# Loading k, its row factors and y two tiles ahead, with six buffers for partial sums, in a hybrid attention and state-space layer

## The chip, the cores and the metric

The kernel runs on one core of one Trainium2 chip. The metric is device time in microseconds (us), the median of several executions; less is better. The core has five engines: TensorE (PE) multiplies matrices, VectorE (DVE), ScalarE (ACT) and GpSimd (POOL) work on tiles of 128 partitions, and SyncE (SP) issues every transfer between device memory (HBM) and the on-chip memory. Each engine works through its own queue in order and waits on semaphores for the others, so an instruction that waits holds up everything behind it on the same engine.

## The reference

One decoder layer on x of 1024 rows and 2048 columns, all in float32:

```python
h = rms_norm(x, ln_gain)
q, k, v, z_att, u, z_ssm, g_att, g_ssm = split(h @ w_in)      # widths 6 x 1024, 2 x 2048
q, k = rms_norm of q and k over each group of 64 channels
attn = (softmax(q1 k1') - lam * softmax(q2 k2')) v            # causal, 8 heads, two maps per head
y_att = rms_norm(attn) * (1 - lam_init) * silu(z_att)
y = gelu(S5 state-space scan of u);  y_ssm = y * sigmoid(y @ w_glu + b_glu) * silu(z_ssm)
merged = sigmoid(g_att) * (y_att @ w_proj_att) + sigmoid(g_ssm) * (y_ssm @ w_proj_ssm)
out = x + merged @ w_out
```

## The kernel before

**Precision.** TensorE multiplies in a rounded float32 format, so each operand is split into a high part (an ACT copy that rounds, L90) and a low part (a DVE subtraction, L91), and a product is three matmuls: high by high, high by low, low by high.

**The input projection.** `h @ w_in` is made in pairs of 128-column blocks: one *pair* gives two blocks of 128 output channels by two halves of 512 rows, that is four result tiles of 128x512. It is done with seven block products in place of eight (a Strassen-Winograd scheme, `pair`, L503 and on). A product is 12 matmuls of 512 columns (L497), so a pair is 84. DVE and ACT make the sums of weight blocks (L346, L366), their high and low parts, and copy or combine the results (u1, u2, u3, p1; L515 to L532, L580 to L591). The contraction of 2048 runs in two halves: a first pass over the 36 pairs leaves partial sums in HBM (`d_p`), and a second pass (`whole`, L543 and on) makes the other half, loads the four partial sums of each pair (tile `q`, L564, from a pool of 5 buffers, L955) and adds them. The trace puts the second pass of z_ssm at about 1320 to 1400 us, then g_att, then g_ssm, to about 1700 us.

**What is done with each result tile.** `whole` hands each finished tile to a function by its kind:

- k: the raw tile is stored to `d_k`, and the sums of its squares are gathered by small matmuls (`norms`). The row factors of all k, one number for each 64 channels and row, go to `d_rk` (`qk_norms`).
- z_ssm: `evac_gate` takes a sigmoid (tile `sg`), loads the matching tile of the state-space output `y` from `d_yg` (one buffer, tag `ks`), multiplies on DVE (L1051) and on POOL (L1052), and stores.
- g_att and g_ssm: a sigmoid in place, and a store (L1055).

**The delayed normalization of k.** `norms_k` (L1012 to L1033) is a generator of 16 steps. One is taken after each of the last 16 pairs in the program's text. A step loads a raw k tile (`ks`, L1017) and its row factors (`rb`, two broadcast loads of 64 partitions each, L1020), multiplies them on DVE (L1028), splits the product (ACT `sh_`, DVE `sl_`) and stores both parts to `d_k0` and `d_k1` (L994). `ks` and `rb` have one buffer each, so the next tile's factors can be loaded only once the multiplication is done, and the next tile only once the split is.

**What sets the order.** The program is written tile by tile. A planner then places the instructions of each engine in a fixed order by its own estimate of times; the attention stage alone has TensorE's order written by hand. The buffers and the waits follow from the pools. So a change in loads or buffers moves instructions that the text does not touch, and the 16 steps of `norms_k` need not stand one to a pair.

Of the kernel before, what the change touches and what calls it, by code (L numbers as in the profile page):

```python
# [10 lines left out]
F32 = mybir.dt.float32  # L11
# [8 lines left out]
P = 128  # L20
# [47 lines left out]
def hybrid_block(ctx: ExitStack, tc: tile.TileContext, x_t, x_n, w_t, w_v, w_glu, w_pa, w_ps,  # L68
                 w_out, small, lams, ssm_bc, out):
    nc = tc.nc  # L70
    V, A, Q, T, D = nc.vector, nc.scalar, nc.gpsimd, nc.tensor, nc.sync
# [17 lines left out]
    def split(hi, lo, src, eng=None):  # L89
        A.activation(hi, src, AF.Copy)  # L90
        (eng or V).tensor_tensor(lo, src, hi.bitcast(F32), ALU.subtract)  # L91
# [11 lines left out]
    def newton_rsqrt(pool, y, v, n):  # L103

        s = pool.tile(list(v.shape), F32, name=n + "_s", tag=n + "_s", bufs=1)
        yi = y.bitcast(I32)
        V.tensor_scalar(yi, v.bitcast(I32), 1, None, ALU.arith_shift_right)
        V.tensor_scalar(yi, yi, -1.0, float(0x5F3759DF), ALU.mult, ALU.add)
        for _ in range(4):
            V.tensor_tensor(s, y, y, ALU.mult)  # L110
            V.tensor_tensor(s, s, v, ALU.mult)
            V.tensor_scalar(s, s, -0.5, 1.5, ALU.mult, ALU.add)
            V.tensor_tensor(y, y, s, ALU.mult)
# [111 lines left out]
    d_yg = dram.tile([8, P, S], F32, name="d_yg")  # L225
# [100 lines left out]
    with ExitStack() as pa_ctx:  # L326
# [230 lines left out]
        def whole(n, a, k, done, qp, rbc=None, w=None):  # L557

            at = ((0, 0), (0, 1), (1, 1), (1, 0))
            qs = {}  # L560
            if rbc is None:
                for i in range(4):
                    qs[i] = qp.tile([P, 512], F32, name="q", tag="q")
                    D.dma_start(qs[i], d_p[n, i])  # L564

            def other(i):
                if i not in qs:
                    c = i // 2
                    q = qp.tile([P, S], F32, name="q", tag="xr", bufs=8)
                    for t in range(2):  # L570
                        m = 2 * c + (t if c == 0 else 1 - t)
                        qs[m] = q[:, t * 512:(t + 1) * 512]
                        D.dma_start(qs[m], d_p[n, m])
                    V.tensor_tensor(q, q, rbc, ALU.mult)
                return qs[i]
            e = Q if rbc is None else V

            def first(ps):
                q = other(0)
                V.tensor_tensor(q, ps, q, ALU.add)  # L580
                done(*at[0], q)

            def second(ps, u):
                e.tensor_tensor(u, u, other(1), ALU.add)  # L584
                V.tensor_tensor(u, ps, u, ALU.add)
                done(*at[1], u)

            def taken(i):
                def f(ps, u):
                    e.tensor_tensor(u, u, other(i), ALU.subtract)  # L590
                    V.tensor_tensor(u, ps, u, ALU.subtract)  # L591
                    done(*at[i], u)
                return f
            pair(w or load_pair(w_s(n, k)), a, first, second, taken(2), taken(3))
# [357 lines left out]
        ev_ctx = ExitStack()  # L952
        stg = ev_ctx.enter_context(tc.tile_pool(name="stg", bufs=2, side="right"))
        more.append(stg)
        qp = ev_ctx.enter_context(tc.tile_pool(name="qp", bufs=5, side="right"))  # L955


        rq = const.tile([P, 16, NT], F32, name="rq")
# [4 lines left out]
        def qk_norms():  # L963

            for t in range(2):
                v = stg.tile([32, 512], F32, name="nv", tag="sq")
                y = stg.tile([32, 512], F32, name="ny", tag="rb", bufs=1)
                V.tensor_scalar(v, nps[t][0:32], 1.0 / 64, EPS, ALU.mult, ALU.add)
                newton_rsqrt(stg, y, v, "nr")
                D.dma_start(d_rk[:, t * 512:(t + 1) * 512], y[16:32])  # L970
                yield
                tp = sps.tile([P, 4, 32], F32, name="rqp", tag="tr", bufs=2)
                for j in range(4):
                    T.transpose(tp[:, j], y[:, j * P:(j + 1) * P], ident[0:32, 0:32])
                V.tensor_copy(rq[:, :, 4 * t:4 * t + 4].rearrange("p a t -> p t a"), tp[:, :, 0:16])
            V.tensor_scalar(nrq, rq, -1.0, None, ALU.mult)
# [15 lines left out]
        def store2(dst, hi, lo):  # L992
            for d_, s_ in zip(dst, (hi, lo)):
                D.dma_start(d_, s_.bitcast(F32))  # L994

        def split_tiles():
            return (stg.tile([P, 512], F32R, name="sh_", tag="sh_"),
                    stg.tile([P, 512], F32R, name="sl_", tag="sl_", bufs=1))
# [13 lines left out]
        def norms_k():  # L1012

            def load(n):
                h, t = divmod(n, 2)
                st = stg.tile([P, 512], F32, name="ks", tag="ks", bufs=1)
                D.dma_start(st, d_k[h, :, t * 512:(t + 1) * 512])  # L1017
                rb = stg.tile([P, 512], F32, name="rb", tag="rb", bufs=1)
                for c in range(2):
                    D.dma_start(rb[64 * c:64 * c + 64],  # L1020
                                d_rk[2 * h + c:2 * h + c + 1, t * 512:(t + 1) * 512].to_broadcast([64, 512]))
                return st, rb
            ahead = load(0)
            for n in range(16):
                yield
                h, t = divmod(n, 2)
                st, rb = ahead
                V.tensor_tensor(st, st, rb, ALU.mult)  # L1028
                hi, lo = split_tiles()
                split(hi, lo, st)  # L1030
                store2([d[h, :, t * 512:(t + 1) * 512] for d in d_ks], hi, lo)
                if n < 15:
                    ahead = load(n + 1)  # L1033

        def evac_v(h, t, st):
            tp = sps.tile([P, 512], F32, name="vt", tag="tr", bufs=2)
# [3 lines left out]
            split(hi, lo, tp)  # L1040
            store2([d[h, :, t * 512:(t + 1) * 512] for d in d_vs], hi, lo)

        def evac_gate(dst, silu, src=None):
            def f(i, t, st):
                if silu:
                    sg = stg.tile([P, 512], F32, name="sg", tag="sq")
                    A.activation(sg, st, AF.Sigmoid)
                    if src is not None:
                        y = stg.tile([P, 512], F32, name="y", tag="ks", bufs=1)
                        D.dma_start(y, src[i, :, t * 512:(t + 1) * 512])  # L1050
                        V.tensor_tensor(st, st, y, ALU.mult)  # L1051
                    Q.tensor_tensor(st, st, sg, ALU.mult)  # L1052
                else:
                    A.activation(st, st, AF.Sigmoid)
                D.dma_start(dst[i, :, t * 512:(t + 1) * 512], st)  # L1055
            return f

        evacs = {"q": evac_q, "k": evac_k, "v": evac_v, "za": evac_gate(d_za, True), "zs": evac_gate(d_zs, True, d_yg),
                 "ga": evac_gate(d_ga, False), "gs": evac_gate(d_gs, False)}
        first = {kind: i for kind, i, _ in KINDS}  # L1060
        for i, (kind, n) in enumerate(order):
            f, m = evacs[kind], n - first[kind]
            whole(n, a, 0, lambda c, t, st, f=f, m=m: f(2 * m + c, t, st), qp, None, w)
            w = None
            if n == 9:
                steps = qk_norms()
            if n in (9, 11, 13):
                next(steps, None)
            if i == 20:
                ks = norms_k()  # L1070
            if i >= 20:
                next(ks, None)

        def yg_inputs(t, raw):
            def ld(k, hi, lo):
                r = raw()
                D.dma_start(r, d_yg[k, :, t * 512:(t + 1) * 512])
                split(hi, lo, r)
            return ld

        def gate_weights(ct):
            ws = []
            for b in range(2):
                raw = wp.tile([P, 4, P], F32, name="w_raw", tag="w_raw", bufs=5)
                D.dma_start(raw, w_glu[ct, :, 4 * b:4 * b + 4])
                m = (2 * ct + b) % 6
                hi, lo = (wp.tile([P, 4, P], F32R, name=n, tag=f"{n}{m}") for n in ("w_hi", "w_lo"))
                split(hi, lo, raw)
                ws.append((hi, lo))
            return ws  # L1090
        ahead = gate_weights(0)
# [55 lines left out]
        load = yg_inputs(1, lambda: gl.tile([P, 512], F32, name="ya", tag="ya", bufs=4))  # L1147
        for k in range(8):
            load(k, ya[1][0][k], ya[1][1][k])
        for ct in range(8):  # L1150
            ws, ahead = ahead, gate_weights(ct + 1) if ct < 7 else None
# [28 lines left out]
    with ExitStack() as at:  # L1180
# [133 lines left out]
        with tc.manual_schedule(engines={T.engine}):  # L1314
            for h in range(H):
# [3 lines left out]
                for n, tt in enumerate(ORDER):  # L1319
                    i = h * NT + n  # L1320
# [172 lines left out]
```

## Time and profile before

| | |
|---|---|
| time, median of 3 executions | 2738.85 us (2737.41 to 2740.82) |
| the profiled execution: its own time | 2741.47 us |
| its span, first to last instruction | 2739.7 us |
| TensorE matmuls busy | 2675.3 us, 98% |
| DVE / ACT / POOL busy | 67% / 44% / 26% |
| moved by DMA | 483.61 MB, mean 177 GB/s |

The stretch that the change touches lies between about 1300 and 1700 us. In the views below a row of windows gives the stretch, its length, and for each engine the busy time with the number of instructions in brackets, then the granted TensorE clock (1.00 is full), the busy share of the 16 DMA engines and what they moved in GB/s. A row of the timeline gives the start, the duration, engine, line, operation and tiles, and in square brackets the idle time of the engine just before it and what ended that. A row of waits gives who waited for whom: total us, times, longest. The busy time of PE counts overlapping, pipelined matmuls, so idle gaps and the number of matmuls in a stretch say more than the busy share.

### The profile page before, as it was taken

The page shows a single profiled execution, that of the slowest core. Times are in us where ns is not written, and L with a number is a line of the kernel's source. Part 1 is how long each engine was busy: PE and PEld are TensorE (multiplying, and loading weights), DVE is VectorE, ACT ScalarE, POOL GpSimd, SP SyncE. Part 2 cuts the span into 40 slices and gives each one's busy share as a digit, 9 for nine tenths or more (in the row PEclk, how much of TensorE's full clock was granted, in tenths as well). Part 3 has the DMA queues.
Part 4 walks back from the last instruction along what each step waited for, and adds up shares of the span by engine and source line. Part 5 has one row for each costly group of instructions (what it writes and reads, how often), then busy time and mean ns, then how long its engine had stood idle before and what let it go on. Part 6 is the DMA issues. An engine that isn't in the chain of part 4 may idle for free. (4 is left out here: it accounts for less than half of the span.)

```text
span 2739.7 us, 37819 instructions
## 1 busy us (share of the span) xinstructions
PE 2675.3 (98%) x12402; PEld 2197.7 (80%) x12402; DVE 1845.8 (67%) x3512; ACT 1195.8 (44%) x2343; POOL 715.7 (26%) x1085
## 2 busy tenths in 40 slices
PE   9999999999999999999998999999999989999999
PEld 8888788887788877888876788777878878888887
DVE  4998877778777798779876666456767574325432
ACT  6433555554455456434334444445555443223221
POOL 0001855566755012224431222012222200000000
PEclk9999999999999999999999999999999999999999
DMA  9653333333233456465577655976787485545453
GB/s 353 209 194 121 100 116 120 118 116 118 97 116 118 174 174 197 145 202 173 192 236 241 219 163 169 287 230 201 208 246 200 147 289 183 154 131 186 146 159 113
DMA packets 259621, 483.61 MB, mean 177 GB/s; under 512 B 33656, under 2 KB 44224, under 8 KB 259424
## 3 DMA queue, kind: packets, MB, share of 16 engines
q1 hardware_dynamic: 259424, 481.20, 54.7%
q8 instruction: 97, 1.59, 0.2%
q14 instruction: 100, 0.82, 0.1%
HBM read 341.52 MB, written 139.56 MB: 176 GB/s over the span
## 5 line engine op out<-in xcount | busy, mean ns | idle before, releaser
L497 PE MATMUL acc<-ah,w_hi 128*128 128x512 f32 x2128 | 839.7, 395 | 24.5 <-ACT u L532 19.0
L497 PE MATMUL acc<-ah,w_lo 128*128 128x512 f32 x2128 | 839.9, 395 | 0.0
L497 PE MATMUL acc<-al,w_hi 128*128 128x512 f32 x2128 | 838.6, 394 | 0.0
L90 ACT ACTIVATE w_hi<-w_raw 128x512 fp32r<-128x512 f32 x516 | 323.9, 629 | 527.7 <-PE o L1409 240.1
L91 DVE TENSOR_TENSOR w_lo<-w_raw,w_hi 128x512 fp32r<-128x512 f32 x458 | 324.1, 708 | 288.1 <-ACT w_hi L90 279.5
L497 PEld LDWEIGHTS acc<-ah,w_hi 128*128 128x128 f32 x2128 | 401.6, 189 | 116.0 <-ACT u L532 23.5
L497 PEld LDWEIGHTS acc<-ah,w_lo 128*128 128x128 f32 x2128 | 401.3, 189 | 86.8 <-issue 5.4
L497 PEld LDWEIGHTS acc<-al,w_hi 128*128 128x128 f32 x2128 | 401.6, 189 | 83.0 <-issue 2.0
L90 ACT ACTIVATE w_hi<-value 128x512 fp32r<-128x512 f32 x304 | 191.3, 630 | 321.5 <-DVE value L346 192.1
L91 DVE TENSOR_TENSOR w_lo<-value,w_hi 128x512 fp32r<-128x512 f32 x304 | 229.4, 755 | 60.3 <-ACT w_hi L90 52.6
L1409 PE MATMUL o<-w_hi,ml 128*128 128x512 f32 x512 | 199.3, 389 | 0.0
L1409 PE MATMUL o<-w_lo,mh 128*128 128x512 f32 x512 | 199.3, 389 | 0.0
L1409 PE MATMUL o<-w_hi,mh 128*128 128x512 f32 x512 | 195.4, 389 | 0.0
L346 DVE TENSOR_TENSOR value<-w_raw 128x512 f32<-128x512 f32 x152 | 160.5, 1056 | 2.8
L584 POOL TENSOR_TENSOR p<-p,q 128x512 f32<-128x512 f32 x36 | 61.9, 1719 | 379.2 <-DVE acc L525 269.1
L91 POOL TENSOR_TENSOR w_lo<-w_raw,w_hi 128x512 fp32r<-128x512 f32 x58 | 79.1, 1366 | 298.9 <-ACT w_hi L90 235.0
L590 POOL TENSOR_TENSOR u<-u,q 128x512 f32<-128x512 f32 x72 | 101.3, 1407 | 167.7 <-ACT u L519 88.0
L1212 DVE TENSOR_SCALAR_CACHE_REDUCE pe<-s,nrq 128x128 f32<-128x128 f32 (+7 forms) x128 | 100.2, 813 | 56.3 <-PE s L1208 55.5
L288 PE MATMUL pc<-ah,w_hi 128*128 128x512 f32 x256 | 105.9, 414 | 12.3 <-ACT w_hi L90 5.9
L1409 PEld LDWEIGHTS o<-w_hi,mh 128*128 128x128 f32 x512 | 96.1, 188 | 20.0
L1409 PEld LDWEIGHTS o<-w_lo,mh 128*128 128x128 f32 x512 | 96.1, 188 | 19.9
L1409 PEld LDWEIGHTS o<-w_hi,ml 128*128 128x128 f32 x512 | 96.1, 188 | 19.9
(503 smaller groups left out, 4543.6 us busy)
## 6 DMA issues: line engine op xcount, KB each, us to landing
w_raw<-in_w_t_dram SPq DMA_DIRECT2D x288, 256.0 KB
q<-d_p SPq DMA_DIRECT2D x160, 256.0 KB
w_raw<-in_w_out_dram SPq DMA_DIRECT2D x128, 256.0 KB
d_p<-u SPq DMA_DIRECT2D x72, 256.0 KB
w_raw<-in_w_ps_dram SPq DMA_DIRECT2D x64, 256.0 KB
w_raw<-in_w_pa_dram SPq DMA_DIRECT2D x64, 256.0 KB
d_p<-ps SPq DMA_DIRECT2D x52, 256.0 KB
d_p<-p SPq DMA_DIRECT2D x36, 256.0 KB
```

The costliest lines, as they stand in the source:

```text
L90: A.activation(hi, src, AF.Copy)
L91: (eng or V).tensor_tensor(lo, src, hi.bitcast(F32), ALU.subtract)
L288: T.matmul(ps, lhsT=w[:, k % 4], rhs=b[k], start=(k == 0 and n == 0), stop=(k == 7 and n == 2))
L346: V.tensor_tensor(t, x, y, ALU.add)
L497: T.matmul(ps, lhsT=x[:, c], rhs=y[i][j], start=(start and j == 0 and n == 0), stop=(j == 3 and n == 2), skip_group_check=True)
L584: e.tensor_tensor(u, u, other(1), ALU.add)
L590: e.tensor_tensor(u, u, other(i), ALU.subtract)
L1212: V.tensor_scalar(pc[c][:, 0:w], sc[c][:, 0:w], nrq[:, 2 * h + c, tt:tt + 1], None, ALU.mult, ALU.min, accum_out=mx[:, c:c + 1])
L1409: T.matmul(ps[i], lhsT=a[k][:, tt], rhs=w[:, 0], start=(k == 0 and n == 0), stop=(k == KT - 1 and n == 2))
```

## The change

Three loads are moved and given other buffers.

- `norms_k` keeps two tiles in flight. At the start it asks for tiles 0 and 1, and after step n for tile n + 2. The raw k tile uses the tag `nh` and the factors the tag `nl`, of two buffers each, which the sums of squares used before and need no more by then.
- y is loaded by a generator of its own, `y_steps`, in the order in which the results of z_ssm come, also into the two buffers of `nh`. Two tiles are asked for in the text after pair 15, the last one ahead of z_ssm, and each use asks for the tile after next.
- The pool of partial sums `q` has six buffers in place of five. The small tile `ny` gets a tag of its own.

```diff
-        qp = ev_ctx.enter_context(tc.tile_pool(name="qp", bufs=5, side="right"))
+        qp = ev_ctx.enter_context(tc.tile_pool(name="qp", bufs=6, side="right"))
...
-                y = stg.tile([32, 512], F32, name="ny", tag="rb", bufs=1)
+                y = stg.tile([32, 512], F32, name="ny", tag="ny", bufs=1)
...
-                st = stg.tile([P, 512], F32, name="ks", tag="ks", bufs=1)
+                st = stg.tile([P, 512], F32, name="ks", tag="nh")
                 D.dma_start(st, d_k[h, :, t * 512:(t + 1) * 512])
-                rb = stg.tile([P, 512], F32, name="rb", tag="rb", bufs=1)
+                rb = stg.tile([P, 512], F32, name="rb", tag="nl")
...
-            ahead = load(0)
+            ahead = [load(0), load(1)]
...
-                st, rb = ahead
+                st, rb = ahead.pop(0)
                 V.tensor_tensor(st, st, rb, ALU.mult)
                 hi, lo = split_tiles()
                 split(hi, lo, st)
                 store2([d[h, :, t * 512:(t + 1) * 512] for d in d_ks], hi, lo)
-                if n < 15:
-                    ahead = load(n + 1)
+                if n < 14:
+                    ahead.append(load(n + 2))
...
+        def y_steps():
+            for m in range(4):
+                for c, t in ((0, 0), (1, 1), (0, 1), (1, 0)):
+                    y = stg.tile([P, 512], F32, name="y", tag="nh")
+                    D.dma_start(y, d_yg[2 * m + c, :, t * 512:(t + 1) * 512])
+                    y_loads[2 * m + c, t] = lambda y=y: y
+                    yield
+        ahead = y_steps()
...
                     if src is not None:
-                        y = stg.tile([P, 512], F32, name="y", tag="ks", bufs=1)
-                        D.dma_start(y, src[i, :, t * 512:(t + 1) * 512])
+                        y = y_loads[i, t]()
                         V.tensor_tensor(st, st, y, ALU.mult)
+                        next(ahead, None)
...
+            if i == 15:
+                next(ahead)
+                next(ahead)
```

**How the order moves.** The number of instructions stays as it was, and so does POOL's order. TensorE's order differs in two places, where the first matmul of a pair now stands ahead of the last product (12 matmuls) of the pair before it. What moves besides are the steps of `norms_k` on DVE and ACT, and the loads on SP. The line numbers of the changed program are 12 to 15 higher from `evac_gate`'s store on (its L1055 is L1067).

On DVE, in g_att, two steps of `norms_k` before. `ks` is the raw k tile, `sl__` the low part of its product, `w_lo` and `value` are weight blocks of the pairs, `u3` and `p1` result tiles:

```order
L1028 TENSOR_TENSOR ks_15431<-ks_15431,rb_15433 128x512
L91 TENSOR_TENSOR w_lo_15131<-value_15128,w_hi_15130 128x512
L346 TENSOR_TENSOR value_15284<-w_raw_15272,w_raw_15274 128x512
L91 TENSOR_TENSOR sl__15598<-ks_15431,sh__15597 128x512
L591 TENSOR_TENSOR u3_15074<-acc_15048,u3_15074 128x512
L91 TENSOR_TENSOR w_lo_15281<-w_raw_15274,w_hi_15280 128x512
L1028 TENSOR_TENSOR ks_15603<-ks_15603,rb_15605 128x512
```

The last row needs the load that can be issued once the fourth row is done: two rows of other work lie between. The steps of the changed program in about the same place (ks_15608 and ks_15780 are two successive k tiles, ks_15952 the one after them):

```order
L1028 TENSOR_TENSOR ks_15608<-ks_15608,rb_15610 128x512
L591 TENSOR_TENSOR u3_15079<-acc_15053,u3_15079 128x512
L91 TENSOR_TENSOR w_lo_15286<-w_raw_15279,w_hi_15285 128x512
L91 TENSOR_TENSOR sl__15947<-ks_15608,sh__15946 128x512
L1028 TENSOR_TENSOR ks_15780<-ks_15780,rb_15782 128x512
L585 TENSOR_TENSOR p1_14989<-acc_14991,p1_14989 128x512
L91 TENSOR_TENSOR w_lo_15141<-value_15119,w_hi_15140 128x512
L346 TENSOR_TENSOR value_15291<-value_15289,w_raw_15281 128x512
L591 TENSOR_TENSOR u2_15004<-acc_15053,u2_15004 128x512
L91 TENSOR_TENSOR w_lo_15294<-value_15291,w_hi_15293 128x512
L91 TENSOR_TENSOR w_lo_15145<-w_raw_15109,w_hi_15144 128x512
```

Here the split of ks_15608 (fourth row) frees the buffer of ks_15952, whose multiplication comes only after ten more rows: seven shown, then L366, the split of ks_15780 and L580. The planner has also pushed the steps together. From the first multiplication of `norms_k` to the last there are 124 rows of DVE before and 102 rows now; the first stands at the first g_att pair in both, and the last falls about 5.9 pairs later before, and about 4.5 pairs later now.

On SP, the transfers of one step before: the stores of the two parts, the next tile's load, and the factors of the tile after it, among the pairs' loads (`w_raw`, `q`) and stores (`d_ga`):

```order
L994 DMA d_k0_75<-sh__16113 128x512
L994 DMA d_k1_76<-sl__16114 128x512
L1017 DMA ks_16119<-d_k_72 128x512
L1020 DMA rb_16121<-d_rk_92 64x512
L564 DMA q_15438<-d_p_81 128x512
L1055 DMA d_ga_84<-p1_15156 128x512
L1020 DMA rb_16293<-d_rk_92 64x512 x2
L994 DMA d_k0_75<-sh__16285 128x512
```

The same kind of stretch now:

```order
L994 DMA d_k1_76<-sl__16119 128x512
L1017 DMA ks_16124<-d_k_72 128x512
L1020 DMA rb_16298<-d_rk_92 64x512
L1067 DMA d_ga_84<-q_15097 128x512
L340 DMA w_raw_15453<-in_w_t_dram 128x512
L994 DMA d_k0_75<-sh__16290 128x512
L1020 DMA rb_16298<-d_rk_92 64x512
L564 DMA q_15275<-d_p_81 128x512
```

The load behind a step's store is now that of the tile after next (ks_16124 behind the store that belongs to ks_15780), and the store d_k0 that follows belongs to a tile that was loaded one step earlier. The y loads stand where they stood among the other transfers of z_ssm, each now for two tiles later.

More of the change, by code (lines that the diff above doesn't have):

```diff
@@ L1041, in evac_v @@
             store2([d[h, :, t * 512:(t + 1) * 512] for d in d_vs], hi, lo)
+        y_loads = {}
+        def y_steps():
[6 more added lines that the diff above has]
+        ahead = y_steps()
         def evac_gate(dst, silu, src=None):
```

## The prediction

> **What bounds the kernel now.** I read the page first, for the busy shares.
>
> ```profile
> span 2739.7 us, 37819 instructions
> PE 2675.3 (98%) x12402; PEld 2197.7 (80%) x12402; DVE 1845.8 (67%) x3512; ACT 1195.8 (44%) x2343; POOL 715.7 (26%) x1085
> ```
>
> TensorE bounds the whole, so the change can only be worth what TensorE now loses where z_ssm, g_att and k's steps are made. The windows of the projection's matmul line alone show how much that is.
>
> ```profile
> 1300.00:1350.00 50.00, 50.00 (x222) 41.35 (x221) 1.00 0.56 184
> 1350.00:1400.00 50.00, 48.06 (x211) 39.16 (x210) 1.00 0.63 207
> 1400.00:1450.00 50.00, 43.83 (x189) 34.96 (x188) 1.00 0.75 246
> 1450.00:1500.00 50.00, 43.49 (x179) 34.11 (x178) 0.97 0.73 240
> 1500.00:1550.00 50.00, 42.19 (x170) 33.54 (x168) 0.93 0.73 243
> 1550.00:1600.00 50.00, 49.72 (x212) 41.00 (x213) 0.97 0.57 178
> ```
>
> An undisturbed 50 us has 222 matmuls, 0.225 us each (84 to a pair: 19 us). From 1350 to 1600 there are 961 where 1110 would fit: 149 x 0.225 = **33.6 us lost**, 2.5 of it before 1400. What TensorE waited for there:
>
> ```profile
> PE acc L497 <- ACT u L532: 17.8, 8, 4.6
> PE acc L497 <- DVE u L591: 2.6, 2, 1.4
> PE acc L497 <- DVE p L585: 1.9, 1, 1.9
> ```
>
> That is 22.3 us of gaps. The clock column gives (0.03 + 0.07 + 0.03) x 50 = 6.5 us more. The last 4.8 us I take for short hitches around the gaps.
>
> Why ACT's copy is late shows in the timeline around the longest gap (SP, DVE, ACT and PE, from four answers).
>
> ```profile
> 1470.52 0.44 SPq L1017 DMA_DIRECT2D ks<-d_k  x1
> 1475.97 0.69 DVE L1028 TENSOR_TENSOR ks<-ks,rb 128x512 f32<-128x512 f32 x1 [3.20 <-DMA d_ga<-q]
> 1477.41 0.69 DVE L91 TENSOR_TENSOR sl__16458<-ks,sh__16457 128x512 fp32r<-128x512 f32 x1
> 1476.75 0.63 ACT L90 ACTIVATE sh__16457<-ks 128x512 fp32r<-128x512 f32 x1 [4.70 <-issue]
> 1477.89 0.58 ACT L532 ACTIVATE u<-acc 128x512 f32<-128x512 f32 x1
> 1478.53 0.50 PE L497 MATMUL acc<-ah,w_hi 128*128 128x512 f32 x1 [4.58 <-ACT u L532]
> ```
>
> The k tile is asked for at 1470.52 and used at 1475.97, 5.45 us later. DVE stands still for it, ACT stands at the split behind it, and the copy that TensorE needs is queued behind that split. DVE's waits at this line, all 16 steps (the wait is put down to whatever transfer came last, so the named tile matters little):
>
> ```profile
> L1028 DVE TENSOR_TENSOR ks<-ks,rb x16: 692/693/1677, 1403.0 to 1543.6; 128x512 f32<-128x512 f32 x16
>   DMA rb<-d_rk: 15.7, 3
>   DMA ks<-d_k: 13.4, 8
>   DMA d_ga<-q: 7.7, 3
>   DMA q<-d_p: 5.7, 1
>   DMA d_ga<-p: 4.6, 1
> ```
>
> Together 47.1 us, and a step each (1543.6 - 1403.0) / 15 = 9.4 us. This is a loop of latency: multiply, split on ACT and DVE, ask for the next tile, wait some 5.5 us for it. DVE itself has room, as whole pairs show (z_ssm; g_att with three steps; a pair without steps; columns PE, PEld, DVE, ACT, POOL, clock, DMA):
>
> ```profile
> 1359.00:1379.50 20.50, 19.52 (x87) 15.83 (x85) 18.47 (x21) 7.86 (x14) 9.89 (x7) 1.00 0.64 206
> 1470.10:1496.60 26.50, 21.76 (x87) 16.87 (x86) 14.44 (x22) 8.95 (x16) 4.43 (x3) 0.94 0.72 244
> 1598.50:1617.50 19.00, 19.00 (x85) 15.78 (x84) 12.24 (x16) 8.37 (x15) 4.25 (x3) 1.00 0.53 166
> ```
>
> **The change, part by part.**
>
> *k two tiles ahead.* No instruction is added; the loop of 9.4 us now carries two steps, 4.7 us each. DVE's new order wants its 15 intervals within 4.5 pairs, 4.5 x 19 = 86 us, or 5.7 us a step. So latency alone no longer binds, and the 47.1 us at L1028 go. What is late next is the transfers' rate. A pair without steps moves 166 GB/s x 19 us = 3.15 MB; a step adds four tiles' worth, by these issue rows (the two stores are 256 KB each as well):
>
> ```profile
> ks<-d_k SPq DMA_DIRECT2D x16, 256.0 KB
> rb<-d_rk SPq DMA_DIRECT2D x30, 128.0 KB
> d_k<-sh__15081 SPq DMA_DIRECT2D x1, 256.0 KB
> ```
>
> That is 256 + 2 x 128 + 2 x 256 = 1024 KB = 1.05 MB. The stretch has to move 4.5 x 3.15 + 15 x 1.05 = 29.9 MB in 86 us: **348 GB/s**, against 243 now. No row shows this mix sustained at that rate; the nearest are the first 10 us of the steps, the busiest 50 us later on, and one stretch of 3.4 us:
>
> ```profile
> DMA packets 1702, 3.07 MB, mean 307 GB/s; under 512 B 204, under 2 KB 204, under 8 KB 1701
> q1 hardware_dynamic: 1701, 3.07, 92.6%
> DMA packets 6969, 13.87 MB, mean 277 GB/s; under 512 B 816, under 2 KB 816, under 8 KB 6965
> 1502.90:1506.30 3.40, 3.40 (x9) 0.52 0.95 351
> ```
>
> At 307 GB/s the 29.9 MB take 97.4 us, 11.4 over the matmuls. Bounds: with the engines wholly busy, 307 / 0.926 = 332 GB/s, 90.1 us, 4 over; at 277 GB/s, 108 us, 22 over. I take 307, because it was reached with the same kinds of transfers by the same queue, while DVE still stopped at every step. The 86 us of matmuls then stretch to 97.4, and DVE waits at L1028 again, but a fifth as long. The steps end about 1.4 pairs sooner, and those pairs run undisturbed.
>
> *The first two k tiles.* Their buffers are freed by the last two y, so they are asked for about 4 us before use where a landing takes up to 5.5: 1 to 2 us of DVE's time, of which I let 1 reach TensorE.
>
> *y two tiles ahead.* It removes a wait that is small:
>
> ```profile
> DVE q L1051 <- DMA y<-d_yg: 3.9, 3, 2.1
> ```
>
> In z_ssm DVE is busy 18.47 of 20.50 us, so the wait costs TensorE part of the 2.5 us lost before 1400. Without it a pair needs 18.5 us plus ACT's 0.8 us, still about 19: I take 1.5 us of the 2.5 as won, 1 as left (bounds 0 and 2.5). The 16 loads are the same ones; the first two go into an earlier stage, whose DMA share is 0.56, and cost nothing there; were that cover gone, two tiles of 256 KB are 1.7 us at 307 GB/s.
>
> *The sixth buffer.* Partial sums are asked for one use sooner; SP waits less behind POOL:
>
> ```profile
> SPq L564 <- POOL u L590: 52.4, 36, 2.2
> SPq L1020 <- DVE ks L1028: 29.3, 14, 4.3
> ```
>
> SP's waits cost only through late tiles, and before L497 no DMA is named as releaser. I take 0, bounds 0 and the 4.8 us of hitches; what is won here is what lets the queue reach 307 GB/s at all.
>
> *TensorE's order.* In two places one matmul of the next pair stands 12 matmuls earlier. If its weights were late there it would hold up 12 x 0.225 = 2.7 us of others; the weights' splits stand in DVE's and ACT's rows as before, well ahead, so I take 0 (bounds 0 and 2 x 2.7).
>
> *The clock.* The half-speed stretches follow the long gaps (the row at 1502.90 above: clock 0.52 for 3.4 us, after a gap of 2.25 us). With the gaps gone the 6.5 us go with them. [...]
>
> **The sum.** Lost now 33.6; left afterwards 11.4 (transfers) + 1 (first k tiles) + 1 (z_ssm) = 13.4; gain 20.2 us. The rest of the kernel keeps its order and follows 20 us sooner: span 2739.7 to 2719.5. The profiled execution took 2741.5, 1.8 more than its span; the median of the runs, 2738.85, is 2.6 below it. Against that median I predict **2719 us**.
>
> **The rivals.**
>
> *Transfers do not bind.* If 348 GB/s can be had (351 was, for 3.4 us) and the stores lag without harm, only the two small terms stay, with a little more: gain 31, **2708**. Against it: 0.95 busy was never held for 10 us in this mix. [...]
>
> *VectorE becomes the bound.* 4.5 pairs x 12.24 us + 15 steps. A step costs about (14.44 - 12.24) / 3 = 0.7 to 1.4 us (two operations of 0.69), so 76 us of 86. But while POOL works, DVE's operations are longer:
>
> ```profile
> 1404.84 1.78 DVE L91 TENSOR_TENSOR sl__15082<-ks,sh__15081 128x512 fp32r<-128x512 f32 x1
> 1429.63 1.68 DVE L1028 TENSOR_TENSOR ks<-ks,rb 128x512 f32<-128x512 f32 x1 [1.47 <-DMA d_ga<-q]
> ```
>
> Were all like these, 55 + 15 x 3.46 = 107 us, 21 over: gain 33.6 - 23 = 11, **2728**. Most are 0.69 us (median above), which speaks against it.
>
> *The change does not do what it says.* If more transfers in flight make each as much slower, a loop of two steps takes 19 us instead of 9.4, DVE waits as before, and only z_ssm is won: **2737**.
>
> *Slower: SP's order sets the rate.* SP's row now has a step's stores, which wait for ACT and DVE, every 5.7 us ahead of weights and partial sums. If SP, standing at those, cannot move more than the present 243 GB/s, 29.9 MB take 123 us; with the 1.4 pairs that follow (26 us) that is 149 us where now 140.6 pass: 8 us slower, **2746** with z_ssm's gain. It decides below 29.9 / (140.6 - 26) = 261 GB/s. For it: the SP waits above. Against: 277 and 307 GB/s went through the same queue.
>
> **How the numbers follow.** Forecast 0.55 (its own range 2710 to 2729, from the 332 and 277 GB/s bounds); no bound by transfers 0.18; VectorE 0.12; nothing won 0.08; slower 0.07. The range for 8 in 10 is 2708 to 2731. Differences within 0.2% (5.5 us) are about what a measurement of this kernel cannot tell from no change. Faster: 0.55 + 0.18 + 0.12 = 0.85; same 0.08; slower 0.07.
>
> **What would show it.** In the changed profile the waits at L1028 should fall from 47 to about 10 us, and the 15 intervals from 140.6 to some 98 us. DMA share in those should be about 0.9 at 300 GB/s or more. Matmuls per 50 us should be 195 to 205 there and 222 afterwards, with at most one or two clock dips before 1600. y's wait at L1051 should be gone. It is wrong if DVE is busy over 95% between the steps (VectorE), if the share stays near 0.73 with L1028 still waiting 3 us a step (nothing won), or if TensorE's gaps name `w_raw`'s split because its load is late (SP's order).

## The result: about 1% faster, and the profile after

The changed kernel takes 2712.8 us in the median (2707.5 to 2713.8) where the one before took 2739.8 beside it. That is the median of four executions, three of 2737.4 to 2740.8 and one of 4762.9 that does not enter the ratio. The ratio is **0.9895** (95%: 0.9881 to 0.9910), or some 29 us less (25 to 33); the means of the seven executions that are left give 0.9900, 27 us, inside that interval. The forecast was 2719 with a range of 2708 to 2731: direction and range hold, and the gain was set too low, 20 where 29 came.

The busy shares of the page, as they stood in the first fence of the prediction:

```profile
span 2705.6 us, 37807 instructions
PE 2663.8 (98%) x12402; PEld 2190.7 (81%) x12402; DVE 1842.2 (68%) x3512; ACT 1196.6 (44%) x2343; POOL 714.1 (26%) x1085
```

The profiled execution is the quickest one of the changed kernel: its span is 34.1 us shorter than the one before. 29 us of these lie where the change is, as the windows of the projection's matmul line show (stretch, length, PE busy and its matmuls, PEld, clock, DMA share, GB/s; kernel after):

```profile
1350.00:1400.00 50.00, 50.00 (x222) 41.44 (x221) 1.00 0.66 217
1400.00:1450.00 50.00, 48.93 (x212) 39.11 (x212) 1.00 0.97 324
1450.00:1500.00 50.00, 48.76 (x212) 39.10 (x211) 1.00 0.95 307
1500.00:1550.00 50.00, 50.00 (x222) 41.44 (x221) 1.00 0.56 174
1550.00:1600.00 50.00, 50.00 (x222) 41.40 (x222) 1.00 0.52 169
```

Of 1110 matmuls that fit into these 250 us there are now 1090, where 961 were: 20 x 0.225 = 4.5 us are lost in place of 33.6, so 29.1 us are won. The projection's last matmul starts at 1700.1 us in place of 1729.3, which is the same 29 us. The clock column reads 1.00 throughout. The other 5 us of the profiled span come later. Before, two stretches of half clock stood there, which the profiled execution after doesn't show (all engines' windows, kernel before):

```profile
1741.90:1745.30 3.40, 3.34 (x8) 2.70 (x9) 2.08 (x3) 1.27 (x3) 0.00 (x0) 0.51 1.04 330
1854.60:1858.00 3.40, 3.40 (x10) 2.62 (x9) 1.96 (x5) 2.11 (x5) 0.00 (x0) 0.50 0.77 299
```

Those 5 us I don't credit to the change: the other executions of it are 5 to 6 us longer than the profiled one, with a mean clock of 0.996 or 0.997 in place of 0.998.

The steps of `norms_k` themselves, by their multiplication's line (first and last start in us, then what VectorE waited for there):

```profile
L1028 DVE TENSOR_TENSOR ks<-ks,rb x16: 675/684/695, 1395.3 to 1487.2; 128x512 f32<-128x512 f32 x16
  DMA ks<-d_k: 2.1, 2
  DMA q<-d_p: 0.3, 1
```

The waits fell from 47.1 us to 2.4, and the 15 intervals from 140.6 us to 91.9. This is that stretch with all engines (PE, PEld, DVE, ACT, POOL, clock, DMA share, GB/s), and what the transfers moved in it; first the kernel before, for its own 15 intervals:

```profile
1403.00:1543.60 140.60, 122.06 (x505) 96.92 (x504) 90.31 (x124) 54.68 (x97) 26.45 (x18) 0.96 0.75 248
```

And the kernel after:

```profile
1395.30:1487.20 91.90, 89.73 (x387) 71.65 (x385) 73.45 (x103) 43.07 (x77) 22.62 (x15) 1.00 0.98 323
...
DMA packets 16504, 29.71 MB, mean 323 GB/s; under 512 B 2032, under 2 KB 2032, under 8 KB 16497
```

29.7 MB went through, at 323 GB/s and a DMA share of 0.98, while TensorE was busy for 89.73 of 91.90 us and did 387 of the 407 matmuls that fit. VectorE's waits in the stretch (from 1390 to 1495) show one that the kernel before did not have:

```profile
DVE sl__15431 L91 <- DMA d_k<-sl__15259: 3.8, 1, 3.8
DVE sl__17594 L91 <- DMA d_k<-sl__17495: 2.7, 1, 2.7
DVE sl__15947 L91 <- DMA d_k<-sl__15775: 2.3, 1, 2.3
```

`sl_` is the low part of a k tile and has a single buffer. The split of one step must wait until the low part of the step before has been stored. Seven such waits in the whole come to 13.8 us. So the wait moved from the load of a tile to the store of its product, and became less than a third as long.

What TensorE still waits for from 1350 to 1600 us:

```profile
PE acc L497 <- ACT u L532: 1.5, 2, 1.1
PE acc L497 <- DVE p L585: 0.5, 1, 0.5
```

The 0.5 us come from the longest of the stores' waits (VectorE's timeline; idle time and releaser in brackets), behind which the evacuation stands:

```profile
1411.40 0.69 DVE L91 TENSOR_TENSOR sl__15431<-ks,sh__15430 128x512 fp32r<-128x512 f32 x1 [3.78 <-DMA d_k<-sl__15259]
1412.01 0.69 DVE L585 TENSOR_TENSOR p<-acc,p 128x512 f32<-128x512 f32 x1
```

The 1.1 us end with a copy of ACT, and no transfer stands behind it (VectorE's and ACT's timelines):

```profile
1481.26 1.66 DVE L346 TENSOR_TENSOR value<-w_raw 128x512 f32<-128x512 f32 x1
1483.02 0.63 ACT L90 ACTIVATE w_hi<-value 128x512 fp32r<-128x512 f32 x1 [2.27 <-DVE value L346]
1483.55 0.58 ACT L532 ACTIVATE u<-acc 128x512 f32<-128x512 f32 x1
```

VectorE's row runs without a pause from 1475 us on, with two multiplications of k in it. A weight block is late from it, and ACT stands at that block's split while the copy `u` is queued behind. The three gaps are 2.0 of the 4.5 us.

### The profile page after: what moved, and what is told of

Read it like the earlier page. It is cut to its first block, busy times and chain, and to the rows that moved or that the text cites. A ratio compares the mean times of both kernels' runs of the same rounds, so it can differ in the third digit from the quotient of the medians.

```text
span 2705.6 us, 37807 instructions
## 1 busy us (share of the span) xinstructions
PE 2663.8 (98%) x12402; PEld 2190.7 (81%) x12402; DVE 1842.2 (68%) x3512; ACT 1196.6 (44%) x2343; POOL 714.1 (26%) x1085
## 4 chain that ended last, share of the span: by engine, by line
PE 82%; DMA 7%; DVE 6%; issue 2%; POOL 2%; ACT 1%; SPq 0%; DVEq 0%; ACTq 0%; POOLq 0%
PE acc L497 44%; PE o L1424 13%; PE pc L271 6%; PE pc L288 4%; PE acc L476 3%; PE pg L1177 2%; PE op L1257 2%; PE s L1220 2%; DMA w_raw<-in_w_ps_dram 1%; DVE w_lo L91 1%; DMA ya<-d_yg 1%; DMA kl<-d_k 1%; PE tp L1245 1%; PE gp L853 1%; DMA al<-d_ys 1%
```

## The experiments

Theory: the loss of 33.6 us is a loop of latency, one load per step, and what is left after the change is set by the transfers' rate (some 307 GB/s). Rivals: transfers do not bind; VectorE binds; the gain comes from y or from the sixth buffer. The ratios below are against the kernel before on the same chip, with their 95% interval; matmuls of the projection are counted in 1300 to 1400 and 1400 to 1600 us, where 443 and about 885 fit (before: 431 and 748; after: 443 and 863).

### The sixth buffer

Two runs: the buffer added to the kernel before, and taken from the changed one.

```diff
# q6_alone, against before
-        qp = ev_ctx.enter_context(tc.tile_pool(name="qp", bufs=5, side="right"))
+        qp = ev_ctx.enter_context(tc.tile_pool(name="qp", bufs=6, side="right"))
# after_q5, against the changed kernel
-        qp = ev_ctx.enter_context(tc.tile_pool(name="qp", bufs=6, side="right"))
+        qp = ev_ctx.enter_context(tc.tile_pool(name="qp", bufs=5, side="right"))
```

> The kernel before with six buffers of partial sums in place of five, and nothing else. Theory: SyncE's waits for these buffers delay no tile that TensorE needs, so 2738 to 2740 us, no change. Rival (the freed queue is what lets the transfers run faster): 8 us or more off, 2731 or less, with the DMA share between 1400 and 1550 above 0.8.

> The changed kernel with five buffers of partial sums again. Theory: no difference to the changed kernel, 2711 to 2714 us. Rival (the sixth buffer lets the queue reach the high rate): 8 us or more slower, 2721 or more, with the DMA share in the k steps below 0.85.

Alone it measured 1.0007 (0.9996 to 1.0017); without it the change measured 0.9896 (0.9881 to 0.9911), as with it. The stretch of the steps in the changed kernel with five buffers:

```profile
1397.70:1488.00 90.30, 89.03 (x388) 71.86 (x386) 73.36 (x103) 42.96 (x77) 22.23 (x15) 1.00 0.98 328
```

The queue reaches 328 GB/s with five buffers. So the sixth is worth nothing that can be measured, and it is not what lets the queue run faster, as the prediction had it.

### y alone and k alone

y two ahead, k one ahead as before, five buffers. The k tile then no longer shares its buffers with y:

```diff
# y_alone, against the changed kernel
-        qp = ... bufs=6
+        qp = ... bufs=5
...
-                st = stg.tile([P, 512], F32, name="ks", tag="nh")
+                st = stg.tile([P, 512], F32, name="ks", tag="ks", bufs=1)
-                rb = stg.tile([P, 512], F32, name="rb", tag="nl")
+                rb = stg.tile([P, 512], F32, name="rb", tag="rb", bufs=1)
...
-            ahead = [load(0), load(1)]
+            ahead = load(0)
...
-                if n < 14:
-                    ahead.append(load(n + 2))
+                if n < 15:
+                    ahead = load(n + 1)
```

> Only y is loaded two tiles ahead into two buffers; k's tiles have one buffer and are asked for one ahead, and the pool of partial sums has five. Theory (k's load loop carries the gain): y is worth what TensorE lost in the z_ssm stage before g_att, at most 2.5 us, so 2736 to 2738 us; the waits at k's multiplication stay near 47 us and TensorE still loses some 30 us from 1400 to 1560. Rival (y is the larger part, because it also lets VectorE enter g_att early): 2725 or less, with k's waits down by more than 10 us.

It measured 0.9995 (0.9982 to 1.0008), but did not isolate what it should. Steps and matmuls in it:

```profile
L1028 DVE TENSOR_TENSOR ks<-ks,rb x16: 678/692/1666, 1197.9 to 1411.4; 128x512 f32<-128x512 f32 x16
...
1300.00:1400.00 100.00, 86.27 (x352) 68.48 (x351) 0.94 0.79 258
1400.00:1600.00 200.00, 200.00 (x875) 165.34 (x874) 0.99 0.57 184
```

The planner took the steps forward to 1197.9 us, beside z_ssm, and the loss went along with them: 352 matmuls in 1300 to 1400 where 443 fit. With k and y in the same two buffers k's steps cannot begin before the last y, so a shared buffer also orders two streams. That loss of 91 matmuls is 20 us, and from 1200 to 1300 us there are 378 where the kernel before has 417, another 9 us. So the 29 us are lost at another place, with other work beside it: the loss is made by the steps and not by the place.

The next two hold k where it was: its first loads wait for the first sigmoid of g_att.

```diff
# y_held, against y_alone
-                D.dma_start(st, d_k[h, :, t * 512:(t + 1) * 512])
+                ins = D.dma_start(st, d_k[h, :, t * 512:(t + 1) * 512])
+                if n < 1:
+                    after(ins, evened[0])
...
-                    A.activation(st, st, AF.Sigmoid)
+                    evened.append(A.activation(st, st, AF.Sigmoid))
# k_held, against the changed kernel: five buffers, the same hold for n < 2, and
-                        y = y_loads[i, t]()
+                        y = stg.tile([P, 512], F32, name="y", tag="ks", bufs=1)
+                        D.dma_start(y, src[i, :, t * 512:(t + 1) * 512])
                         V.tensor_tensor(st, st, y, ALU.mult)
-                        next(ahead, None)
...
-            if i == 15:
-                next(ahead)
-                next(ahead)
```

> As the run with y alone, but the first k load is held until the first g_att tile has its sigmoid, so that k's steps come after z_ssm as in both kernels. Theory: y's lookahead is worth the 2.5 us of the z_ssm stage and k's loop of latency stays: 2736 to 2738 us, z_ssm loses under 1 us of matmuls, waits at k's multiplication 40 to 50 us. Rival (y's lookahead is worth the 6 us that lie between the run with k alone and the changed kernel): 2734 to 2735.

> Only k's tiles and row factors are loaded two ahead, into two buffers each; y has one buffer as before, the pool of partial sums five. The first two k loads are held until the first g_att tile has its sigmoid, so that the steps start where they do in both kernels. Theory: the loop of load, multiply and split is halved, so nearly the whole gain is here: 2713 to 2717 us, waits at k's multiplication under 6 us, the 15 intervals in 90 to 100 us, DMA share there 0.93 or more. Rival (the gain needs y or the sixth buffer as well): 2725 or more.

y_held measured 0.9994 (0.9983 to 1.0005), k_held 0.9919 (0.9905 to 0.9934), which is 2718.6 us and a little slower than expected. First y_held's matmuls and its waits at the k multiplication:

```profile
1300.00:1400.00 100.00, 100.00 (x443) 82.81 (x442) 1.00 0.61 199
1400.00:1600.00 200.00, 181.71 (x754) 145.77 (x753) 0.96 0.70 226
...
  DMA ks<-d_k: 24.7, 11
  DMA rb<-d_rk: 14.7, 3
  DMA w_raw<-in_w_t_dram: 6.3, 1
  DMA d_ga<-q: 3.1, 1
```

Then k_held's:

```profile
1300.00:1400.00 100.00, 97.57 (x428) 79.86 (x427) 1.00 0.60 194
1400.00:1600.00 200.00, 195.04 (x855) 159.90 (x854) 1.00 0.74 245
...
  DMA ks<-d_k: 4.0, 3
```

With y alone the loop of k's steps stands as it was: 48.8 us of waits, 131 matmuls missing. What y wins is before 1400: 443 matmuls for 431, 12 x 0.225 = 2.7 us, too little to show in the whole. With k two ahead the waits at that line fall to 4.3 us with the other one there, and 22 of the 29 us are won. Against k_held the change with five buffers has 15 matmuls more in either stretch (443 and 870), 3.4 us each, 0.23% together. The two intervals overlap narrowly, and k_held also has the hold, so of the second 3.4 us I can't say whether y or the earlier start of k's loads wins them.

### The tile or its factors

Each step loads a tile and two rows of factors. Either one is put back to one buffer and one step ahead, the other left as in the changed kernel.

```diff
# factors_one, against the changed kernel (load is divided into load_k and load_r)
-                rb = stg.tile([P, 512], F32, name="rb", tag="nl")
+                rb = stg.tile([P, 512], F32, name="rb", tag="rb", bufs=1)
-            ahead = [load(0), load(1)]
+            ahead_k, ahead_r = [load_k(0), load_k(1)], [load_r(0)]
...
+                if n < 15:
+                    ahead_r.append(load_r(n + 1))
# tiles_one, likewise; the first load of a tile waits for the first sigmoid of g_att
-                st = stg.tile([P, 512], F32, name="ks", tag="nh")
+                st = stg.tile([P, 512], F32, name="ks", tag="ks", bufs=1)
-            ahead = [load(0), load(1)]
+            ahead_k, ahead_r = [load_k(0)], [load_r(0), load_r(1)]
...
+                if n < 15:
+                    ahead_k.append(load_k(n + 1))
```

> The changed kernel with one buffer for k's row factors, asked for one ahead as before; the k tiles stay two ahead. Theory (each load has its own loop of latency: a factor's load is asked for right after the multiplication and takes 5 to 8 us, so the loop is some 7 us where the order wants 6): half of the gain goes, waits at the multiplication 10 to 30 us, 2717 to 2728. Rival (the factors never were late, only the tile is): 2711 to 2714.

> The changed kernel with one buffer for the k tiles, asked for one ahead behind the split as before, and held as in the run with y alone; the factors stay two ahead. Theory (the tile's loop of multiply, split, load is the longest, 9.4 us): nearly the whole gain goes but y's 2 us, waits at the multiplication 35 to 50 us, 2732 to 2739. Rival (the factors' loads were what was late): 2722 or less.

factors_one measured 0.9936 (0.9918 to 0.9955), tiles_one 0.9950 (0.9931 to 0.9969). factors_one:

```profile
L1032 DVE TENSOR_TENSOR ks<-ks,rb x16: 679/693/705, 1394.0 to 1502.3; 128x512 f32<-128x512 f32 x16
  DMA rb<-d_rk: 17.6, 8
...
1400.00:1600.00 200.00, 191.49 (x826) 156.57 (x825) 0.98 0.73 237
```

tiles_one:

```profile
L1034 DVE TENSOR_TENSOR ks<-ks,rb x16: 691/693/1596, 1405.3 to 1541.1; 128x512 f32<-128x512 f32 x16
  DMA ks<-d_k: 23.9, 10
...
1400.00:1600.00 200.00, 181.51 (x778) 145.59 (x777) 0.99 0.71 231
```

By most of the waiting time the releaser follows the part that was put back: the factors in the one, the tile in the other. In all 25.5 us of waits stay with one set of factors and 45.3 with one tile (12.1 of these without a releaser in the trace). The time of tiles_one, 2730.8 us, lies just below what was expected. Each load closes a loop of its own. The tile's is the longer, since its buffer comes free only with the split, the factors' already with the multiplication. Measured against y_held's 754 matmuls, the second tile alone wins 72 x 0.225 = 16 us, the second set of factors alone 24 x 0.225 = 5.4; both together win 24.5 (863 - 754 = 109). So neither half of the change would have done by itself.

### Do the transfers bind what is left?

Both parts of each k tile are stored a second time, into tiles of DRAM that nothing reads: 16 x 2 x 256 KB, 8.4 MB more. Nothing else is changed in the text.

```diff
# more_bytes2, against the changed kernel
+    d_kx = [dram.tile([H, P, S], F32, name=f"d_kx{i}") for i in range(2)]
...
-        def store2(dst, hi, lo):
-            for d_, s_ in zip(dst, (hi, lo)):
+        def store2(dst, *parts):
+            for d_, s_ in zip(dst, parts):
...
-                store2([d[h, :, t * 512:(t + 1) * 512] for d in d_ks], hi, lo)
+                store2([d[h, :, t * 512:(t + 1) * 512] for d in d_ks + d_kx], hi, lo, hi, lo)
```

> The changed kernel with both parts of each k tile stored a second time, to a place that nobody reads: two more transfers of 256 KB a step, no other work. The planner lets the 15 intervals take 6.4 pairs then. Theory (the transfers' rate binds in the new steps): 43.9 MB at 323 GB/s take 136 us where the matmuls need 122: 7 to 12 us slower than the changed kernel, 2719 to 2724, DMA share still 0.95 or more. Rival (the rate is high but binds nothing): within 2 us of the changed kernel, 2711 to 2714.

It measured 0.9889 (0.9872 to 0.9905): not slower at all. Its stretch of steps, and the projection's matmuls:

```profile
1395.40:1521.30 125.90, 123.45 (x544) 101.50 (x543) 98.69 (x136) 60.98 (x106) 31.69 (x21) 1.00 1.01 344
...
1400.00:1600.00 200.00, 197.55 (x870) 162.86 (x870) 1.00 0.85 289
```

The transfers ran at 344 GB/s for 126 us, and TensorE did 870 matmuls, not fewer than in the changed kernel. So neither 307 nor 323 GB/s is the most that the queue can move, and the theory in this form falls. What the run does not say is how it would be with the steps as close as they were, or with fewer stores in the mix: the planner, which knows of the added stores, has put them over 6.4 pairs in place of 4.5.

### What is left: the stores' buffer, and how close the steps stand

If rate is not it, the loss left (4.5 us) can be the single buffer of the low part, or the steps that stand so close that VectorE has no room for anything late. sl2 gives the low part a second buffer:

```diff
-                    stg.tile([P, 512], F32R, name="sl_", tag="sl_", bufs=1))
+                    stg.tile([P, 512], F32R, name="sl_", tag="sl_"))
```

> The changed kernel with two buffers for the low parts of k (tile sl_) in place of one, so that VectorE no longer waits (13.8 us in all) for a store of the step before. Theory (the transfers' rate binds, and VectorE has room): within 1.5 us of the changed kernel, 2711 to 2714. Rival (that wait is what TensorE still loses): 2707 to 2709.

It measured 0.9887 (0.9871 to 0.9904), not told apart from the changed kernel. Matmuls, and what VectorE waits for at the multiplication:

```profile
1400.00:1600.00 200.00, 198.35 (x872) 162.82 (x871) 1.00 0.74 243
...
  DMA rb<-d_rk: 7.9, 4
  DMA ks<-d_k: 3.7, 4
```

The store's wait is gone, and the wait at the multiplication comes back, 12.7 us in all (11.6 of them for loads) where 2.4 were. 872 matmuls for 863 is 2 us, too little to build on: after_q5, whose time is that of the changed kernel, has 870. The steps are then made three to two pairs, in two ways. In spread each *load* of a k tile waits for the newest sigmoid of g_att; in spread_mult the loads stay early and the *multiplication* waits for it.

```diff
# both, against the changed kernel
-                    A.activation(st, st, AF.Sigmoid)
+                    evened.append(A.activation(st, st, AF.Sigmoid))
...
             if i >= 20:
                 next(ks, None)
+                if i % 2:
+                    next(ks, None)
# spread
-                D.dma_start(st, d_k[h, :, t * 512:(t + 1) * 512])
+                ins = D.dma_start(st, d_k[h, :, t * 512:(t + 1) * 512])
+                if evened:
+                    after(ins, evened[-1])
# spread_mult
-                V.tensor_tensor(st, st, rb, ALU.mult)
+                after(V.tensor_tensor(st, st, rb, ALU.mult), evened[-1])
```

> The changed kernel with each k load held until the sigmoid of the newest g_att or g_ssm tile, and three steps of k in the text to every two pairs: the 15 intervals stretch over some ten pairs, at 250 GB/s in place of 323. Nothing else changes. Theory (the rest that TensorE still loses, 6 us, is the transfers' rate): 2706 to 2709 us, matmuls lost from 1400 to 1600 under 2 us. Rival (it is the order on VectorE or the single buffer of the low parts): 2711 or more.

> The changed kernel with each multiplication of k, not its load, held until the sigmoid of the newest g_att or g_ssm tile, and three steps to every two pairs: 15 intervals over about ten pairs, the loads still two ahead and early. The run that held the loads waited 57 us at the multiplication because each load came just ahead of its use. Theory (late loads cost, not how the steps are spread): waits at the multiplication under 5 us, matmuls lost from 1400 to 1600 under 4 us, 2706 to 2711. Rival (spreading itself harms, for instance by longer use of VectorE beside POOL): 2716 or more, with the waits small.

spread measured 0.9928 (0.9913 to 0.9943), worse than the change, and for a reason that neither its theory nor its rival names:

```profile
L1030 DVE TENSOR_TENSOR ks<-ks,rb x16: 680/692/694, 1409.9 to 1597.4; 128x512 f32<-128x512 f32 x16
  DMA ks<-d_k: 56.5, 10
...
1400.00:1600.00 200.00, 190.81 (x823) 154.50 (x822) 0.99 0.70 233
```

spread_mult measured 0.9878 (0.9860 to 0.9895):

```profile
L1028 DVE TENSOR_TENSOR ks<-ks,rb x16: 684/692/694, 1423.4 to 1613.8; 128x512 f32<-128x512 f32 x16
...
1423.40:1613.80 190.40, 190.40 (x841) 157.66 (x840) 142.50 (x191) 91.27 (x155) 43.19 (x30) 1.00 0.76 246
```

The steps stand equally far apart in both, about ten pairs for 16. Held at the load, a tile lands just when it is used, or later: 56.5 us of waits. Held at the use, VectorE does not wait for a load at this line at all, and TensorE is busy for all of its 190.40 us. The low part has its single buffer here, and VectorE waits 10.2 us for its stores in all, at no cost to TensorE. So what is lost in the changed kernel is most likely lost because the steps stand close, and the stores' wait costs only there. The matmul counts say so (863, 870 and 872 with close steps, 884 here); the times of the changed kernel and of spread_mult can't be told apart. The holding itself costs nothing that shows; it has to be on the use. spread also shows what a wait costs. Its 57 us over ten pairs took (885 - 823) x 0.225 = 14 us from TensorE; before, 47 us over some six pairs took 31 by the same count (137 matmuls). A pair without steps leaves VectorE idle for 19 - 12.24 = 6.8 us, and the sizes fit if only what goes beyond that idle time reaches TensorE. An estimate: 5.9 pairs leave 40 us, the 16 steps use 22 of these (two operations of 0.69 us each), so 47 - 18 = 29 us should be lost before, and 31 are; ten pairs leave 68, so 57 - 46 = 11 in spread, where 14 are. factors_one (five pairs, 25.5 us of waits) comes to 14 for 13 measured, tiles_one (5.9 pairs, 45.3 us) to 27 for 24.

The last run puts the two together, the held multiplication and the second buffer for the low part.

> The run with the multiplications spread, and two buffers for the low parts of k as well. Theory: TensorE has nothing left to lose here (it lost 1.6 us with one buffer), so the same as with one buffer, a ratio to the kernel before of 0.987 to 0.989, 2706 to 2710 us, and no wait of VectorE for a store of the step before. Rival (the stores' buffer still costs): 2703 to 2705.

It measured **0.9868** (0.9846 to 0.9891), 2704.3 us in the median. That time lies in the rival's range, and the ratio just under the theory's. Its matmuls:

```profile
1400.00:1600.00 200.00, 200.00 (x884) 165.58 (x884) 1.00 0.74 244
```

884 of 885 matmuls: nothing is lost in this stage. spread_mult has 884 from 1400 to 1600 too (the 1.6 us that the expectation has it lose are not in this count), so by the matmuls the second buffer adds nothing there. By the times the intervals overlap, and it is not settled. It is the fastest of all the kernels by its ratio and clearly faster than the one before. Its interval overlaps that of the changed kernel, so the further gain of 5 us by the matmuls (21 x 0.225 = 4.7; 3 us against after_q5's 870) and of 7 us by the ratios (0.27% of 2739) is not settled either.

## Why the prediction was right in direction and too small

**The loop of latency: right, and shown.** Take away one of its two loads' second buffers and the wait comes back at that load (17.6 us for factors, 23.9 for tiles); take away both and 48.8 us stand there. Moved beside z_ssm, the steps lose the same 29 us there. With both two ahead 2.4 us are left.

**What is late next: the step that failed.** The prediction said "What is late next is the transfers' rate", took 307 GB/s from 10 us of the steps before, and let 11.4 us be lost. (Those are 1410 to 1420 us; the first 10 us, 1403 to 1413, moved 284 GB/s.) Bytes were right (29.9 MB foreseen, 29.7 moved), and the intervals came near (97.4 foreseen, 91.9 measured); but the reading that the transfers could do no more was not. 323 GB/s passed in the changed kernel, 344 over 126 us with more stores, which is also above the 332 that were taken as the bound for wholly busy engines. The profile before could have shown it: the 50 us from 1750 that gave the bound of 277 GB/s hold 17.5 us in a row at 388, with other loads and stores, as its 40 slices of 1.25 us show (busy share of the transfer engines in tenths, 9 is 90% or more, and the rate):

```profile
DMA  9999999999999999999999789988949630872059
GB/s 223 203 166 205 206 213 216 259 408 388 390 383 395 402 405 385 329 402 402 411 370 357 211 303 295 310 288 326 334 167 365 141 113 0 320 243 67 0 200 295
```

The 307 were reached while VectorE stopped at every step, and I used it as if it were what the queue could give. The term measured 4.5 us in place of 11.4, and its nature is another: 16 steps within 4.5 pairs leave VectorE and ACT little room for a store that lands late or an operation of 1.66 us. These are the gaps that the trace names, 2.0 of the 4.5 us; the rest has no name. Spaced over ten pairs with the loads early, the loss is gone from the matmul counts. The longest of the stores' waits ends 6.2 us after that store's issue at 1405.24 us; whether the DMA share of 0.98 makes stores late was not tried by itself.

**The rival "transfers do not bind"** had the mechanism that the runs bear out, with late stores left open. Its 2708 lies 4.8 us below the 2712.8 measured and the forecast 6.2 above: it left "the two small terms" and a little more, where 4.5 were lost for another reason.

**The first k tiles** were to cost 1 us. VectorE waited 1.1 us for the second of them, at 1399.3 us, and TensorE, with 443 matmuls in 1300 to 1400, nothing: VectorE's idle time took it.

**y:** forecast 1.5 of 2.5 us, 1 left; measured 2.7 won in y_held before 1400 and nothing left, as no matmul is missing there in the changed kernel either. Over the whole, y_held is not told apart from no change.

**The sixth buffer:** 0 was right, the sentence that it lets the queue reach 307 GB/s was wrong (328 without it).

**The clock:** the 6.5 us were to go, and did. The four half-speed stretches between 1479 and 1554 have no successor between 1300 and 1600 (clock 1.00).

**VectorE as the bound:** it is busy for 73.45 of 91.90 us, 80%, and its operations in the steps have a median of 0.684 us. This falls. **"Nothing won" and "slower by SP's order"** fall too: DMA share 0.98 in place of 0.75, and no gap of TensorE names a weight whose load is late.

**Signs that were named:** L1028's waits about 10 us (2.4), intervals 98 (91.9), share 0.9 at 300 GB/s (0.98 at 323), 195 to 205 matmuls per 50 us (212), 222 afterwards (222), at most two dips (none), y's wait gone (gone). All went the way foreseen, most beyond the size.

## What to carry to other kernels

When the rows of a stage show one load after another, each asked for only when the tile before is done, count the loop's length against the step that the other engines would allow, and give every load in that loop its second buffer: with one of two left out, about 60% (one set of factors) or half (one tile) of the gain came. A rate that was measured while some engine was standing still may be only what was asked for, and not what can be had (here 307 GB/s with VectorE stopping at every step, 323 where it waited 2.4 us in all, 344 with more stores); a limit of rate is looked for by adding bytes. After such a change look for the next single buffer in the same loop, and if work has to be spaced out, hold the use and leave the load early (0.9878 against 0.9928 here).

## What was not expected of the hardware

The DMA share stood at 0.98 and 1.01 for 92 and 126 us, at 323 and 344 GB/s, while TensorE lost 20 of 407 matmuls (5%) in the one stretch and 14 of 558 (3%) in the other. A share near 1 by itself was no sign of a bound here. Nor did it fix the rate: from 1750 to 1760 us before, the slices above show 166 to 259 GB/s, and from 1760 to 1777.5 they show 329 to 411, all of them at a share of 0.9 or more.

The four half-speed stretches of the steps before are each 3.4 us long (PE's windows, clock in the next to last but one column; the one at 1502.90 stands in the prediction):

```profile
1479.10:1482.50 3.40, 3.40 (x10) 0.50 0.86 299
1526.90:1530.30 3.40, 3.12 (x7) 0.50 0.84 302
1550.80:1554.20 3.40, 3.40 (x9) 0.50 0.68 226
```

From one start to the next it is 23.8, 24.0 and 23.9 us. Just ahead of them TensorE's timeline of the kernel before has the four longest gaps of the steps: 4.58, 2.25, 3.61 and 2.24 us, with ends at 1478.53, 1502.65, 1527.18 and 1550.28 us, which are 24.1, 24.5 and 23.1 us apart. Two of the gaps are shorter than the stretch behind them. The next longest, 1.88 us with its end at 1441.51 us, has no such stretch behind it: the clock reads 1.00 from 1441.5 to 1478.5 us. Why half speed came behind the four, no run shows.
